# End of a recurrence in a hybrid decoder trunk: head norm in smaller parts, y turned and split in halves, two gate pieces last

## The chip, the core and the metric

The kernel runs on one core of a Trainium2 chip. The metric is the time of one execution on the device in microseconds (us), as the median of several runs. The engines are TensorE (PE, with PEld for its weight loads), VectorE (DVE), ScalarE (ACT), GpSimd (POOL) and SyncE (SP), which issues most DMAs. Line numbers (L112) are those of the kernel before.

## The reference

One layer of a decoder trunk on 1024 positions of width 1024, in float32. The input is normalized and projected once; the columns of the projection go to three branches and their gates. A branch is a recurrence over time (8 heads of 64), causal attention, or attention into 256 memory tokens. The branches are gated and merged, projected by w_out, and a convolutional feed-forward part follows.

```python
h = rms_norm(x, norm1_g[l])
proj = h @ w_in[l]
p_rwkv, p_sb, q_mem, gate_logits = jnp.split(proj, cut, axis=-1)
y_a, v_first = rwkv7_branch(p_rwkv, ...)
y_b = stick_breaking_branch(p_sb, ...)
y_m = memory_branch(q_mem, mem, ...)
ys = jnp.stack([y_a, y_b, y_m], axis=2)
branch_out = jnp.einsum('btnc,ncd->btnd', ys, w_branch[l])
gates = jax.nn.sigmoid(gate_logits.reshape(b, t, N_BRANCH, D_MODEL))
x = x + jnp.sum(gates * branch_out, axis=2) @ w_out[l]
x = x + conv_ffn(x, norm2_g[l], ...)
```

What matters here is the end of the first branch: the output y of the recurrence is normalized per head over 64 columns (mean and variance), scaled by lnx_g, shifted by lnx_b and a bonus term, and multiplied by a gate.

## The kernel before

A float32 matrix is split into a high and a low part, and each product takes three matmuls: high by high, high by low, low by high. PE runs nearly all of the time, and its order is written by hand: as long as `self.pin` is set, matmuls and transposes keep the order in which the program emits them. The order of the other engines is planned when the kernel is built: an instruction goes to its engine's list when the planner's clock says that its data and its buffer are there, earlier program text first.

The work before the merge is laid out as a main strand and a filler. The filler (`stream`, drawn through `pumped`) is a list of pieces of projections: a piece of 128 columns is eight steps of six matmuls of 512 columns (a gate piece, `gate_item`), or four such steps (a branch piece, `branch_item`). The main strand is a generator, and `weave` draws so many filler steps at each of its yields: 2.08 in the recurrence (`stage2`), 3 in `group_norm`. What is then left of the filler is drained. Each piece's weights are loaded one piece ahead by SP into one of two "wr" slots, and split by ACT (high part, L80) and POOL (low part, L81).

The recurrence (`stage2`) runs through 16 chunks of 64 positions, with three yields a chunk, for four tiles y[p] of two heads each (128 rows by 1024 columns: the rows are the positions of two chunks, and each group of 128 columns is one such pair of chunks for the two heads). After every fourth chunk `norm_quarter` normalizes the 256 columns that are then complete, in all four tiles: four reduces on DVE (L566), a scaling (L567), 16 squares with a running sum on ACT (L573), a power on POOL (L166, helper rsqrt), and 16 scalings of 64 columns on DVE (L580). It is a generator of ten steps, drawn one at a time at the yields of the next chunks. The last quarter follows chunk 15, drawn two steps at a yield, five yields in all.

`group_norm` turns a tile: eight transposes of 128 x 128 on PE (L105) into two PSUM banks, two multiplies by the loaded scale on DVE (L597), and one add of the loaded shift over 1024 columns (L598). Scale and shift come from DRAM by SP (L606, L607) into "at" buffers, of which there are seven. `branch_last` splits the turned tiles into a high part (ACT, L1094, in "at") and a low part (DVE, L1095, in "A", four buffers, which the low parts of branch 2 hold until its last matmul). Then it runs eight pieces of 128 columns with 24 matmuls each; DVE multiplies the result by the stored gate (L1183) and adds what the other branches gave (L1184), and ACT and DVE split it for w_out (L1190, L1191). `out_proj` follows, with its eight rows of w_out split into the slots that `load_wo` names. The text from `branch_last` to `out_proj` is not pinned.

A gate piece ends in a sigmoid. If its number (branch, piece) is in `stored`, ACT's queue stores it to DRAM (gsd, L738), and the branch piece that needs it loads it (L1117); if not, it stays in a "w4" buffer until its branch piece, which comes right behind it. The list `gq` gives the order in which the stored ones are made. A branch piece of branch 2 also loads the sum so far (mrd, L1120), multiplies (DVE, L1132), adds (POOL, L1134) and stores (POOL's queue, L1135). There are three "w4" buffers.

Of the kernel before, what the change touches and what calls it, by code (L numbers as in the profile page):

```python
# [49 lines left out]
class Trunk:  # L50
# [421 lines left out]
    def stage2(self):  # L472
        nc = self.nc
# [32 lines left out]
        for c in range(NC):  # L506
            g, cc = c // 2, c % 2
            us = []
            for p in range(4):
                L, (V, TT) = Ls[g, p], VTs[g, p]  # L510
                us.append((
                    U[p], L[:, cc * 128 : (cc + 1) * 128], L[:, 256 + cc * 128 : 256 + (cc + 1) * 128],
                    L[:, 512 + cc * 256 : 512 + (cc + 1) * 256], [v[:, cc * 64 : (cc + 1) * 64] for v in V],
                    TT[:, cc * 64 : (cc + 1) * 64], v1s[p], self.ps("g")))

            def state(o, rs):
                for p, h2 in heads if c else ():
# [12 lines left out]
            for p, h2 in heads:  # L530
                _, _, _, _, wv, tt, v1, pb = us[p]
                self.mmul(pb[hq[1 - h2], W], tt[hq[h2]], v1[hq[h2]], start=True, stop=True)
                if h2 == 1:
                    for q, w in zip(hq, wv[::-1]):
                        nc.scalar.activation(w[q], pb[q, W], AF.Copy)
            yield
            next(norm, None)
            state(Y, A)
            for p, (Up, ra, bt, M, wv, tt, v1, pb) in enumerate(us):
                for h2, q in enumerate(hq):  # L540
                    self.mmul(pb[q, Y], M[:, h2 * 128 : h2 * 128 + 64], wv[h2], start=(c == 0), stop=True)
                if c < NC - 1:
                    for h2, q in enumerate(hq):
                        self.mmul(pb[q, S], bt[:, q], wv[h2], start=True, stop=True)
                    nc.vector.scalar_tensor_tensor(Up, Up, self.pc[p][:, c : c + 1], pb[:, S], ALU.mult, ALU.add)
                for h2, q in enumerate(hq):
                    nc.scalar.activation(self.y[p][cc * 64 : cc * 64 + 64, g * 128 + h2 * 64 : g * 128 + h2 * 64 + 64], pb[q, Y], AF.Copy)
            if cc and g + 2 < NG:
                for p in range(4):
                    load(g + 2, p)  # L550
            yield
            next(norm, None)
            if c % 4 == 3:
                for _ in norm:
                    pass
                norm = self.norm_quarter(c // 4)
        for _ in norm:
            next(norm, None)
            yield

    def norm_quarter(self, i):
        nc = self.nc
        nm, vs = self.small("hn", [128, 16]), self.small("hn", [128, 16])
        ys = [y[:, i * 256 : (i + 1) * 256] for y in self.y]
        for p, y in enumerate(ys):
            nc.vector.tensor_reduce(nm[:, p * 4 : p * 4 + 4], y.rearrange("p (g i) -> p g i", i=64), AX.X, ALU.add)  # L566
        nc.vector.tensor_scalar(nm, nm, -1.0 / 64, None, ALU.mult)  # L567
        yield
        groups = [[(y[:, j * 64 : (j + 1) * 64], p * 4 + j) for j in range(4)] for p, y in enumerate(ys)]
        for gs in groups:  # L570
            for y, j in gs:
                junk = self.small("jk", [128, 64], bufs=1)
                nc.scalar.activation(junk, y, AF.Square, bias=nm[:, j : j + 1], accum_out=vs[:, j : j + 1])  # L573
            yield
        rs = self.small("hf", [128, 16], bufs=4)
        self.rsqrt(rs, vs, 16, 1.0 / 64, 64e-5)
        yield
        for gs in groups:
            for y, j in gs:
                nc.vector.tensor_scalar(y, y, nm[:, j : j + 1], rs[:, j : j + 1], ALU.add, ALU.mult)  # L580
            yield

    def group_norm(self):
        nc = self.nc
        self.yT, gs = [], []
        for p in range(3):
            gs.append(self.load_gg(p))
        yield
        for p in range(4):
            y = self.y[p]  # L590
            gg, bg = gs[p]
            for h in range(2):
                hs = slice(h * 512, (h + 1) * 512)
                pt = self.ps("g")
                for j in range(4):
                    self.transpose(pt[:, j * 128 : (j + 1) * 128], y[:, (h * 4 + j) * 128 : (h * 4 + j + 1) * 128])
                nc.vector.tensor_tensor(gg[:, hs], pt, gg[:, hs], ALU.mult)  # L597
            nc.vector.tensor_tensor(y, gg, bg, ALU.add)  # L598
            self.yT.append(y)
            if p == 0:  # L600
                gs.append(self.load_gg(3))
            yield

    def load_gg(self, p):
        gg, bg = self.t4("at"), self.t4("at")
        self.nc.sync.dma_start(gg, self.ggd[p, 0])  # L606
        self.nc.sync.dma_start(bg, self.ggd[p, 1])  # L607
        return gg, bg
# [472 lines left out]
                mid(s - 2)  # L1081
            yield

    def split_y(self, ys, last=False):
        nc = self.nc
        if last:
            his = [self.t4("at", F32R) for _ in ys]
        else:
            hi = self.pool_a.tile([128, 4, 1024], F32R, name=self.nm("yhi"), tag="inst")
            his = [hi[:, k] for k in range(4)]  # L1090
        out = []
        for hi, y in zip(his, ys):
            lo = self.t4("A", F32R)
            nc.scalar.activation(hi, y, AF.Copy)  # L1094
            nc.vector.tensor_tensor(lo, y, hi.bitcast(F32), ALU.subtract)  # L1095
            out.append((hi, lo))
        return out
# [51 lines left out]
        return load, items  # L1149

    def load_wo(self, k):
        slots = ["qk"] * 8 + ["at"] * 6 + ["it", "sp"]
        hl = [self.pool_l.tile([128, 1024], F32R, name="wo_sp", tag="sp", bufs=1) if s == "sp" else self.t4(s, F32R) for s in slots[2 * k : 2 * k + 2]]
        self.wo.append(self.split_raw(self.load_w(self.I["w_out"][k]), *hl))

    def branch_last(self):
        nc = self.nc
        self.wo = []
        y = self.split_y(self.yT, True)
        mg = lambda name, shape: self.pool_l.tile(shape, F32R, name=name, tag="l4")  # L1160
        self.mg0 = [[mg(f"mg0_{i}_{k}", [128, 2, 512]) for k in range(4)] for i in range(2)]
        self.mg1 = [[[mg(f"mg1_{i}_{t}_{k}", [128, 4, 256]) for k in range(2)] for t in range(2)] for i in range(2)]
        for d in range(8):
            if d % 2 == 0:
                w = self.split_w(self.I["w_br"][0, d // 2])
            g, o = self.t4("at"), self.t4()
# [1 line left out]
            nc.sync.dma_start(o, self.mrd[d])  # L1168
            pp = [self.ps("mm"), self.ps("mm")]
            if d == 0:  # L1170
                for i, (a, b) in enumerate(((0, 0), (1, 0), (0, 1))):
                    for k in range(4):
                        for h in range(2):
# [515 lines left out]
    def run(self):  # L1689
        nc, tc = self.nc, self.tc  # L1690
# [153 lines left out]
```

## Time and profile before

| what | us |
|---|---|
| median of 3 runs | 1870.23 |
| lowest, highest | 1868.52, 1876.17 |
| profiled execution | 1869.02 |
| its span, first to last instruction | 1867.2 |
| PE busy in the span | 1799.3 |
| mean granted TensorE clock | 0.988 |

A profile shows one execution. A timeline row gives start, length, engine, line, operation, output and inputs, the count of instructions merged into the row, and in brackets how long the engine was idle before and who released it. A row of the groups gives line, engine, operation, shapes and count, then the busy time and the mean length of one in ns, then the idle time of the engine just before. A row by stretch gives its length and the busy time of PE, PEld, DVE, ACT and POOL with the number of instructions, then the granted clock (1.00 is full), the DMA share and GB/s. A row of the DMA view gives target and source, queue, count, size of one, and the median time to landing.

### The profile page before, as it was taken

To read this page: it belongs to the slowest core of one execution; us is meant where nothing else is said; L and a number is where in the kernel's file an instruction comes from. 1 tells how busy PE (TensorE), PEld (TensorE's weight loads), DVE (VectorE), ACT (ScalarE), POOL (GpSimd) and SP (SyncE) were. 2 spreads that over 40 slices of the span, in tenths; PEclk is the share of its full clock that TensorE was granted. 3 is DMA by queue.
4 is the path that set the end of the run, shared out by engine and by line. 5 is a ranking of instruction groups with operands and counts; after the bars stand their busy time and mean duration, and the time that the engine had idled before them with its cause. 6 is when DMAs were issued, how large, how long until landed. Compare 5 with 4: busy or idle time off the path is not lost. (4 is left out here: it accounts for less than half of the span.)

```text
span 1867.2 us, 27381 instructions
## 1 busy us (share of the span) xinstructions
PE 1799.3 (96%) x10468; PEld 1451.9 (78%) x10468; DVE 1163.3 (62%) x1638; ACT 885.8 (47%) x1665; POOL 787.1 (42%) x448
## 2 busy tenths in 40 slices
PE   8999999999999999999999899979999999999999
PEld 6777778878787887787777688767888888878877
DVE  5656665998887423333333682467777677785586
ACT  5444343555565635534545433454444444554433
POOL 2323342322222452122233431487676767645454
PEclk9999999999999999999999999999999999999999
DMA  4155565111111432557744463222333233385475
GB/s 177 57 176 174 177 210 157 60 51 44 46 59 63 133 116 64 181 191 269 251 134 173 167 231 110 91 90 90 108 113 102 86 124 106 120 323 202 140 240 188
DMA packets 120037, 261.29 MB, mean 140 GB/s; under 512 B 28249, under 2 KB 40793, under 8 KB 119778
## 3 DMA queue, kind: packets, MB, share of 16 engines
q1 hardware_dynamic: 82434, 193.71, 31.7%
q10 hardware_dynamic: 33696, 53.23, 7.8%
q0 software_dynamic: 3776, 12.62, 2.1%
q8 instruction: 82, 1.34, 0.3%
q14 instruction: 49, 0.40, 0.1%
HBM read 178.99 MB, written 80.48 MB: 139 GB/s over the span
## 5 line engine op out<-in xcount | busy, mean ns | idle before, releaser
L81 POOL TENSOR_TENSOR wl<-wr,wh 128x1024 fp32r<-128x1024 f32 x77 | 195.2, 2536 | 499.3 <-ACT wh L80 499.2
L112 PE MATMUL mm<-xhi,wh 128*128 128x512 f32 x784 | 265.0, 419 | 9.6 <-ACT xhi L179 7.9
L112 PE MATMUL mm<-xlo,wh 128*128 128x512 f32 x784 | 246.6, 396 | 0.2 <-DVE xlo L180 0.2
L112 PE MATMUL mm<-xhi,wl 128*128 128x512 f32 x784 | 244.1, 393 | 0.4 <-POOL wl L81 0.3
L112 PEld LDWEIGHTS mm<-xlo,wh 128*128 128x128 f32 x784 | 149.3, 191 | 34.1 <-DVE xlo L180 0.9
L112 PEld LDWEIGHTS mm<-xhi,wl 128*128 128x128 f32 x784 | 148.5, 190 | 34.4 <-POOL wl L81 1.3
L112 PEld LDWEIGHTS mm<-xhi,wh 128*128 128x128 f32 x784 | 138.6, 192 | 40.5 <-issue 9.1
L80 ACT ACTIVATE wh<-wr 128x1024 fp32r<-128x1024 f32 x77 | 81.4, 1057 | 158.3 <-PE mm L112 84.5
L112 PE MATMUL mm<-dw,da 128*128 128x512 f32 x528 | 121.2, 390 | 1.5 <-DVE da L1584 1.4
L112 PE MATMUL mm<-BT,l 128*128 128x512 f32 x504 | 117.6, 389 | 0.0
L112 PE MATMUL mm<-BT,wh 128*128 128x512 f32 x352 | 110.0, 394 | 7.8 <-DVE u L1397 7.8
L112 PEld LDWEIGHTS mm<-dw,da 128*128 128x128 f32 x528 | 98.8, 188 | 23.3 <-DVE da L1584 2.3
L1585 POOL TENSOR_TENSOR dw<-draw,dw 128x512 fp32r<-128x512 f32 x55 | 81.1, 1482 | 84.8 <-ACT dw L1583 82.0
L831 DVE TENSOR_TENSOR_SCAN at<-at,at 128x128 f32<-128x128 f32 (+3 forms) x64 | 91.3, 1429 | 32.0 <-ACT at L825 31.9
L112 PE MATMUL mm<-B,wh 128*128 128x512 f32 x352 | 108.4, 389 | 2.1 <-ACT p L1439 2.1
L112 PEld LDWEIGHTS mm<-BT,l 128*128 128x128 f32 x504 | 94.6, 188 | 19.6
L1584 DVE TENSOR_TENSOR da<-draw,da 128x512 fp32r<-128x512 f32 x77 | 65.6, 860 | 61.2 <-ACT da L1582 60.6
L112 PE MATMUL g<-dw,da 128*128 128x512 f32 x396 | 92.2, 394 | 3.0 <-ACT dw L1583 1.9
L733 DVE TENSOR_TENSOR w<-w,rbc 128x1024 f32<-128x1024 f32 x24 | 49.2, 2049 | 68.7 <-ACT w L732 63.9
L1345 POOL TENSOR_TENSOR l<-it,l 128x1024 fp32r<-128x1024 f32 x21 | 50.8, 2419 | 95.3 <-ACT l L1344 95.3
L112 PEld LDWEIGHTS g<-dw,da 128*128 128x128 f32 x396 | 75.3, 190 | 19.4 <-ACT dw L1583 2.3
L1582 ACT ACTIVATE da<-draw 128x512 fp32r<-128x512 f32 x77 | 48.3, 628 | 83.8 <-PE mm L112 39.9
(326 smaller groups left out, 4002.2 us busy)
## 6 DMA issues: line engine op xcount, KB each, us to landing
wr<-in_w_in_dram SPq DMA_DIRECT2D x50, 512.0 KB, 3.6
draw<-actd SPq DMA_DIRECT2D x77, 256.0 KB, 3.6
at<-scr SPq DMA_DIRECT2D x28, 512.0 KB, 5.8
draw<-in_w_down_dram SPq DMA_DIRECT2D x55, 256.0 KB, 4.6
wr<-in_w_up_dram SPq DMA_DIRECT2D x22, 512.0 KB, 3.5
actd<-gall ACTq DMA_DIRECT2D x44, 256.0 KB, 3.0
rw<-in_w_up_dram SPq DMA_DIRECT2D x20, 512.0 KB, 3.7
gsd<-w ACTq DMA_DIRECT2D x18, 512.0 KB, 2.7
```

Source lines behind the costliest of these rows:

```text
L80: self.nc.scalar.activation(hi, raw, AF.Copy)
L81: self.nc.gpsimd.tensor_tensor(lo, raw, hi.bitcast(F32), ALU.subtract)
L112: self.pinned(self.nc.tensor.matmul(*a, **k))
L733: nc.vector.tensor_tensor(g, g, self.rbc, ALU.mult)
L831: self.pinned(nc.vector.tensor_tensor_scan(sn[:, :W][:, ::-1], sn[:, :W][:, ::-1], self.smask[:, 1024 - W :][:, ::-1], 1.0, ALU.mult, ALU. ...
L1345: nc.gpsimd.tensor_tensor(lo, src, hi.bitcast(F32), ALU.subtract)
L1582: self.pinned(nc.scalar.activation(A[:, 0], a, AF.Copy))
L1584: self.pinned(nc.vector.tensor_tensor(A[:, 1], a, A[:, 0].bitcast(F32), ALU.subtract))
L1585: nc.gpsimd.tensor_tensor(Wt[:, 1], w, Wt[:, 0].bitcast(F32), ALU.subtract)
```

## The change

The last quarter of the head norm becomes two parts. The norm now runs after chunks 3, 7, 11, 13 and 15, for column groups 0-1, 2-3, 4-5, 6 and 7, and what is left of a part when the next begins is issued at once. After chunk 13 the scale and shift of tiles 0 and 1 are loaded. The five yields behind chunk 15 go.

`group_norm` works in halves of 512 columns: first it turns half 0 of all four tiles (the add on POOL), then splits half 0 (high part in "qk", low part in "A"), then turns and splits half 1 tile by tile (the add on DVE). It has eleven yields, with one filler step at each. The fourth shift takes the "it" slot. `branch_last` takes these parts, and its first piece does columns 0 to 511 before 512 to 1023. `load_wo` uses the slots in another order. The gate pieces (2,2) and (2,3) are made among the stored ones, and (0,6) and (0,7) come last, behind branch 2.

```diff
-            if c % 4 == 3:
+            if c in (3, 7, 11, 13, 15):
                 for _ in norm:
                     pass
-                norm = self.norm_quarter(c // 4)
+                norm = self.norm_part(*{3: (0, 2), 7: (2, 4), 11: (4, 6), 13: (6, 7), 15: (7, 8)}[c])
+            if c == 13:
+                self.gs = [self.load_gg(p) for p in range(2)]
         for _ in norm:
-            next(norm, None)
-            yield
+            pass
...
     def group_norm(self):
         nc = self.nc
-        self.yT, gs = [], []
-        for p in range(3):
-            gs.append(self.load_gg(p))
+        gs = self.gs + [self.load_gg(2), self.load_gg(3, True)]
+        hl = [(self.t4("qk", F32R), self.t4("A", F32R)) for _ in range(4)]
+        self.yhl = hl
+
+        def turn(p, h, eng):
+            hs, (gg, bg), y = slice(h * 512, (h + 1) * 512), gs[p], self.y[p]
+            pt = self.ps("g")
+            for j in range(4):
+                self.transpose(pt[:, j * 128 : (j + 1) * 128], y[:, (h * 4 + j) * 128 : (h * 4 + j + 1) * 128])
+            nc.vector.tensor_tensor(gg[:, hs], pt, gg[:, hs], ALU.mult)
+            eng.tensor_tensor(y[:, hs], gg[:, hs], bg[:, hs], ALU.add)
+
+        def split(p, h):
+            hs, (hi, lo) = slice(h * 512, (h + 1) * 512), hl[p]
+            nc.scalar.activation(hi[:, hs], self.y[p][:, hs], AF.Copy)
+            nc.vector.tensor_tensor(lo[:, hs], self.y[p][:, hs], hi[:, hs].bitcast(F32), ALU.subtract)
+
         yield
         for p in range(4):
...
-            nc.vector.tensor_tensor(y, gg, bg, ALU.add)
-            self.yT.append(y)
-            if p == 0:
-                gs.append(self.load_gg(3))
-            yield
...
+            turn(p, 0, nc.gpsimd)
+            if p % 2:
+                yield
+        for p in range(4):
+            split(p, 0)
+            yield
+        for p in range(4):
+            turn(p, 1, nc.vector)
+            split(p, 1)
+            yield
...
-        slots = ["qk"] * 8 + ["at"] * 6 + ["it", "sp"]
+        slots = ["qk"] * 4 + ["at"] * 4 + ["qk"] * 4 + ["at"] * 2 + ["it", "sp"]
...
-        y = self.split_y(self.yT, True)
+        y = self.yhl
...
-                for i, (a, b) in enumerate(((0, 0), (1, 0), (0, 1))):
-                    for k in range(4):
-                        for h in range(2):
+                for h in range(2):
+                    for i, (a, b) in enumerate(((0, 0), (1, 0), (0, 1))):
+                        for k in range(4):
...
-        gq[14:14] = [(2, 0), (2, 1)]
+        gq[14:14] = [(2, d) for d in range(4)]
...
-        items += [lambda: drain(inv), ld1, gate(), gate(), gate(), mark("y1"), *br1, ld2, gate(), *br2]
+        items += [lambda: drain(inv), ld1, gate(), gate(), gate(), mark("y1"), *br1, ld2, gate(), *br2, gate(), gate()]
...
-        self.weave(self.group_norm(), pump, 3, 0)
+        self.weave(self.group_norm(), pump, 1.0, 0)
```

`norm_part(g0, g1)` is `norm_quarter` with 2 * (g1 - g0) heads' columns of 64 per tile in place of four, and reduce, scaling and power over as many.

More of the change, by code (lines that the diff above doesn't have):

```diff
@@ L575, in norm_quarter @@
         rs = self.small("hf", [128, 16], bufs=4)
-        self.rsqrt(rs, vs, 16, 1.0 / 64, 64e-5)
+        self.rsqrt(rs[:, : 4 * nh], vs[:, : 4 * nh], 4 * nh, 1.0 / 64, 64e-5)
         yield
@@ L584, in group_norm, with load_gg @@
         nc = self.nc
-        self.yT, gs = [], []
-        for p in range(3):
-            gs.append(self.load_gg(p))
+        gs = self.gs + [self.load_gg(2), self.load_gg(3, True)]
[12 more added lines that the diff above has]
+            nc.vector.tensor_tensor(lo[:, hs], self.y[p][:, hs], hi[:, hs].bitcast(F32), ALU.subtract)
         yield
         for p in range(4):
-            y = self.y[p]
-            gg, bg = gs[p]
-            for h in range(2):
[L593 to L598, printed above, removed]
-            self.yT.append(y)
-            if p == 0:
-                gs.append(self.load_gg(3))
-            yield
-    def load_gg(self, p):
-        gg, bg = self.t4("at"), self.t4("at")
+            turn(p, 0, nc.gpsimd)
[3 more added lines that the diff above has]
+            split(p, 0)
+            yield
+        for p in range(4):
+            turn(p, 1, nc.vector)
+            split(p, 1)
+            yield
+    def load_gg(self, p, last=False):
+        gg, bg = self.t4("at"), self.t4("it", n=1080)[:, :1024] if last else self.t4("at")
         self.nc.sync.dma_start(gg, self.ggd[p, 0])
@@ L1082, in mem_attn, with split_y @@
             yield
-    def split_y(self, ys, last=False):
+    def split_y(self, ys):
         nc = self.nc
[L1086 to L1090, printed above, removed]
+        hi = self.pool_a.tile([128, 4, 1024], F32R, name=self.nm("yhi"), tag="inst")
+        his = [hi[:, k] for k in range(4)]
         out = []
@@ L1170, in branch_last @@
             if d == 0:
-                for i, (a, b) in enumerate(((0, 0), (1, 0), (0, 1))):
-                    for k in range(4):
-                        for h in range(2):
+                for h in range(2):
+                    for i, (a, b) in enumerate(((0, 0), (1, 0), (0, 1))):
+                        for k in range(4):
                             self.mmul(pp[h], w[a][:, k * 256 : k * 256 + 128], y[k][b][:, h * 512 : (h + 1) * 512],
```

13 lines of the change are left out of this document (7 added, 6 removed).

## The prediction

> **What bounds the kernel now.** The page comes first: one core, and TensorE is the busy engine.
>
> ```profile
> span 1867.2 us, 27381 instructions
> PE 1799.3 (96%) x10468; PEld 1451.9 (78%) x10468; DVE 1163.3 (62%) x1638; ACT 885.8 (47%) x1665; POOL 787.1 (42%) x448
> ```
>
> PE is idle for 1867.2 - 1799.3 = 67.9 us in all, so a reordering can win only where PE waits or runs at a lower clock. The change touches the stretch from the end of the recurrence to the first branch; there the view of waits (waiter, releaser, total, times, longest) names who PE waits for.
>
> ```profile
> ACT at L1094 <- DVE qk L598: 7.4, 3, 2.6
> PE mm L112 <- ACT at L1094: 5.2, 3, 3.2
> ```
>
> Read backwards: PE waits for the high-part copy of y (ACT, L1094), which waits for the DVE add that finishes y (L598). The groups of PE from 1058.05 to 1080.42, and busy times by stretch (length, then PE, PEld, DVE, ACT, POOL, granted clock, DMA):
>
> ```profile
> L112 PE MATMUL mm<-at,wh 128*128 128x512 f32 x14 | 5.8, 539 | 5.2 <-ACT at L1094 5.2
> L112 PE MATMUL mm<-at,wl 128*128 128x512 f32 x12 | 4.9, 550 | 0.0
> L112 PE MATMUL mm<-A,wh 128*128 128x512 f32 x14 | 4.2, 428 | 1.0 <-DVE A L1095 1.0
> L105 PE MATMUL g<-kon,qk 128*128 128x128 f32 x16 | 2.3, 279 | 0.3 <-DVE at L597 0.3
> ```
>
> ```profile
> 1058.06:1080.43 22.37, 15.79 (x57) 11.08 (x56) 16.98 (x16) 6.89 (x7) 14.39 (x6) 0.77 0.69 233
> 1080.43:1114.88 34.45, 34.45 (x153) 28.53 (x152) 32.84 (x48) 13.09 (x26) 10.36 (x4) 1.00 0.67 229
> 1070.00:1075.00 5.00, 3.72 (x8) 2.52 (x9) 4.56 (x3) 1.30 (x2) 1.13 (x1) 0.50 0.93 298
> ```
>
> ```profile
> 1028.91 0.73 PE L112 MATMUL mm<-xhi,wh 128*128 128x512 f32 x2
> ...
> 1050.83 1.03 PE L105 MATMUL g<-kon,qk 128*128 128x128 f32 x8
> 1051.62 0.71 PE L112 MATMUL mm<-yhi,wh 128*128 128x512 f32 x2
> ...
> 1070.04 2.07 PE L112 MATMUL mm<-at,wh 128*128 128x512 f32 x4 [3.22 <-ACT at L1094]
> ```
>
> In the timeline of PE, 1028.91 is the first matmul behind the recurrence's last. What the stretch from 1058.06 costs: 40 matmuls (14 + 12 + 14) and 16 transposes took 22.37 us. At full clock a matmul of 512 columns takes 34.45 / 152 = 0.2266 us (one of the 153 is cut by the edge), and eight transposes 1051.62 - 1050.83 = 0.79 us. The same work needs 40 x 0.2266 + 2 x 0.79 = 10.65 us, so **11.7 us are lost**: 5.2 + 1.0 + 0.3 = 6.5 of waiting, and some 5.2 because the clock is at 0.50 after the 3.22 us gap. This is the ceiling for what a better end can give.
>
> [...]
>
> **The change, part by part.**
>
> *Where the cover goes.* One step of the pump is six matmuls, 6 x 0.2266 = 1.36 us. Groups of PE from 1028.90 to 1058.05 (three kinds of x24, three of x16; first and last):
>
> ```profile
> L112 PE MATMUL mm<-xhi,wh 128*128 128x512 f32 x24 | 7.5, 394 | 0.0
> L112 PE MATMUL mm<-A,wh 128*128 128x512 f32 x16 | 4.9, 390 | 0.0
> ```
>
> 72 + 48 = 120 matmuls: **20 steps** are left when the recurrence ends, and before, 16 of them stand ahead of the first transposes, so 4 are left for the rest. With the change 2 follow the last chunk, then one at each of group_norm's 11 yields, then 7. The PE order becomes: 3 steps, turn of half 0 of two tiles, 1, of the other two, 5, then four times (turn of half 1, 1 step), then 7. The turns of half 0 come at about 1028.9 + 3 x 1.36 = 1033; the first turn of half 1 after 9 steps and 16 transposes of 128 columns, at 1028.9 + 12.2 + 1.6 = **1042.7**; branch_last's first matmul at 1028.9 + 20 x 1.36 + 4 x 0.79 = **1059.3** (before: 1060.4). Since gates (0,6) and (0,7) close the stream, branch 2 ends with step 4 and frees the four A tiles that the low parts need, at about 1036. The number of matmuls, and of gate columns, is the same: (2,2) and (2,3) move ahead by what (0,6) and (0,7) fall back.
>
> *Is half 1 normalized in time?* Nothing in the trace is a last part of one column group; it is built from the last quarter's rows:
>
> ```profile
> 1029.15 1.83 DVE L566 TENSOR_REDUCE hn<-qk 128x4 f32<-128x256 f32 x4 [7.29 <-ACT qk L547]
> L573 ACT ACTIVATE jk<-qk,hn 128x64 f32<-128x64 f32 x16 | 5.6, 347 | 1.1 <-DVE hn L567 0.7
> L573 ACT ACTIVATION_READ_ACCUMULATOR jk<-qk,hn 128x1 f32 x16 | 3.0, 187 | 0.0
> L166 POOL TENSOR_TENSOR hf<-rs,half 128x16 f32<-128x16 f32 x1 | 2.9, 2927 | 1.8 <-DVE rs L165 1.8
> L166 POOL TENSOR_TENSOR hf<-rs,half 128x8 f32<-128x8 f32 x5 | 8.3, 1668 | 30.3 <-DVE rs L165 30.2
> 1044.92 5.74 DVE L580 TENSOR_SCALAR qk<-qk,hn,hf 128x64 f32<-128x64 f32 x16 [2.45 <-POOL hf L166]
> ```
>
> Before: reduces from 1029.15, scaling until 1044.92 + 5.74 = 1050.7, so 21.5 us. New: four reduces 0.9 to 1.8 (half the columns), eight squares 8 x (0.347 + 0.187) = 4.3, the power 1.7 (eight columns), and of the scalings only the first two for the first turn, 2 x 5.74 / 16 = 0.7; two more DVE steps on a few columns cost less than a reduce (0.46 each). That is 7.6 to 9.4, from 1029.15 to 1037 or 1039. Other work of these engines in between, two ACT copies or one POOL split (rows below: 2.1, 2.6), makes 1041. Against 1042.7: **no wait**; bounds 0 to 2.6 us. The extra part in chunks 14 and 15 adds four reduces and eleven short steps beside the recurrence; most of it stands in place of work that came later, and I take 0.3 us (0 to 2).
>
> *Turn and split.* Uncontended rows, and the nearest one for the add that moves to POOL:
>
> ```profile
> L597 DVE TENSOR_TENSOR at<-g,at 128x512 f32<-128x512 f32 x4 | 2.6, 684 | 0.8 <-PE g L105 0.8
> L598 DVE TENSOR_TENSOR qk<-at,at 128x1024 f32<-128x1024 f32 x2 | 2.4, 1216 | 0.0
> L1585 POOL TENSOR_TENSOR dw<-draw,dw 128x512 fp32r<-128x512 f32 x55 | 81.1, 1482 | 84.8 <-ACT dw L1583 82.0
> L598 DVE TENSOR_TENSOR qk<-at,at 128x1024 f32<-128x1024 f32 x4 | 7.9, 2003 | 0.0
> ```
>
> Half 1 of a tile costs DVE the multiply, 0.68, the add and the low part's subtraction (an instruction of the same form), half of 1.22 each: 1.9 us, 7.6 for four, from 1042.7 on, and the last turn is at 1048.0: ready at about 1051, while the seven steps last until 1059.3. The first piece of branch_last now takes columns 0 to 511 first (12 matmuls, 2.7 us), so half 1 may come as late as 1062. Half 0's splits lie wholly under the steps before. The cover is 8 us; if it is gone, each us beyond it is a us of PE. The reason for late data would be DVE against POOL: the last row is the add of the second one over all four tiles, at a mean of 2003 ns; in the stall POOL is busy 14.39 of 22.37 us. POOL gains four adds, 4 x 1.48 = 5.9 us. I take 0.7 us of PE loss (0 to 6).
>
> [...]
>
> *Loads.* load_gg of tiles 0 and 1 moves up into chunk 13, two loads each on SP, where it stands ahead of the next mrd and w_br loads and waits for the at buffers of chunks 12 and 13 to come free, so SP cannot issue it much earlier than before; those behind it have a piece, 8 us (below), to land. The fourth bias takes the "it" slot and no longer waits for a free "at". Two more gate stores (ACT's queue) and two more gate loads (SP), 512 KB each, are wanted a piece or more later. I take 0 for all; a load that is late by its whole landing costs what the starved pieces do.
>
> *w_out slots.* Rows 4 and 5 of w_out now sit in the slots of the high parts of y, free only when branch_last's last matmul is done:
>
> ```profile
> 1114.88 11.36 PE L112 MATMUL mm<-qk,mg 128*128 128x512 f32 x48
> 1126.08 8.32 PE L112 MATMUL mm<-at,mg 128*128 128x512 f32 x36
> 1115.90 5.20 POOL L81 TENSOR_TENSOR at<-wr,at 128x1024 fp32r<-128x1024 f32 x2 [2.34 <-ACT at L80]
> wr<-in_w_out_dram SPq DMA_DIRECT2D x8, 512.0 KB, 3.8
> L80 ACT ACTIVATE wh<-wr 128x1024 fp32r<-128x1024 f32 x77 | 81.4, 1057 | 158.3 <-PE mm L112 84.5
> ```
>
> The first w_out matmul is at 1114.88. Row 4 is wanted 48 matmuls after that, 11.2 us. An ACT copy of 1.1 and POOL at 2.6 each make rows 4 and 5 ready after 3.7 and 6.3; row 6 follows a load of 3.8 and another 3.7, at 11.2, wanted at 16.4. Cost 0 (to 8 if POOL or the queue slips), cover 5 us.
>
> Sum: -11.7 + 0.3 + 0.7 = **-10.7 us**. The profiled execution took 1869.0 us (span 1867.2); this gives 1858.3 there, and from the median 1870.2 it gives **1859.5**.
>
> **The rivals.**
>
> *Starved pieces of branch 2 (slower).* Pieces (2,0) to (2,3) now follow each other with stored gates; before only two did. Each needs two w4 buffers of three.
>
> ```profile
> 902.06 0.73 PE L112 MATMUL mm<-yhi,wh 128*128 128x512 f32 x2
> 910.26 0.73 PE L112 MATMUL mm<-yhi,wh 128*128 128x512 f32 x2
> 909.82 2.39 POOL L1134 TENSOR_TENSOR w<-w,w 128x1024 f32<-128x1024 f32 x1 [5.60 <-DVE w L1132]
> 920.48 2.37 POOL L1134 TENSOR_TENSOR w<-w,w 128x1024 f32<-128x1024 f32 x1
> mrd<-w POOLq DMA_DIRECT2D x16, 512.0 KB, 5.2
> w<-mrd SPq DMA_DIRECT2D x16, 512.0 KB, 6.0
> ```
>
> PE needs 910.26 - 902.06 = 8.2 us a piece. If multiply (two halves at L597's 0.68), add 2.4, store 5.2 and load 6.0 of one piece must pass before the next, that is 15.0, a slip of 6.8 for three successions, 20.4; PSUM's four banks hide one piece, 8.2. PE then idles 12.2, and at the ratio of the stall above (11.7 lost for 6.5 waited) loses 22: 1869.0 - 10.7 + 22 = 1880, in the median 1881. Against it: the two that stood together were 10.66 us apart on POOL, a slip of 2.5, 7.4 for three, less than 8.2. It decides from 2.7 us of slip a piece.
>
> [...]
>
> *The wait only moves.* PE stands still at the first piece as before, since DVE and POOL have the same work to do in fewer us: 1870. For it: DVE is 4.56 of 5.00 busy in the stall. Against it: seven steps of cover.
>
> *w_out late.* PE waits up to 8 us at row 4 or 6: 1867.5.
>
> **How the numbers follow.** About 0.5% (9.4 us, below 1860.9) can be told from no change. Forecast 0.62, its own range 1857 to 1862.5, of which 0.55 is beyond 0.5%; half 1 late 0.14 (0.01 of it beyond 0.5%); only moved 0.07; w_out late 0.05; starved pieces 0.12 (0.02 within 0.5%). So faster 0.55 + 0.01 = 0.56, slower 0.10, within 0.5% 0.07 + 0.13 + 0.07 + 0.05 + 0.02 = 0.34. The range 1856.5 to 1869.0 leaves out the starved pieces, part of "only moved" and the lower edge of the forecast, about 0.18.
>
> **What would show it.** Right: no PE wait for the copies of y, the granted clock at 1.00 from the recurrence's end to w_out, the first-branch matmuls begin some 30 us after the last recurrence matmul and run 43.5 us without a gap. The norm step: the last scaling ends before 1045. [...] Wrong: PE waiting at (2,2) to (2,4) for a multiply; a wait of a turn for the last scaling; a PE gap at row 4 of w_out; or a total near 1870 with the wait at a new line.

## The result, and the profile after

| | median us | lowest, highest | ratio to before (95% interval) |
|---|---|---|---|
| before | 1873.15 (19 runs beside the changed kernel) | 1866.8, 1877.1 | 1 |
| changed | 1879.68 (19 runs) | 1871.9, 1884.0 | 1.0036 (1.0025 to 1.0048) |

The changed kernel is **slower by 0.36%**, 6.5 us between the medians; 10.7 us of gain were forecast. Line numbers of the changed kernel are shifted: L566 is now L568 (reduces), L573 L575 (squares), L580 L582 (scalings), L597 and L598 L596 and L597 (multiply and add of a turn), L1094 and L1095 L601 and L602 (high and low parts of y), L1132, L1134, L1135 are L1142, L1144, L1145 (multiply, add and store of a piece of branch 2), L1183, L1184, L1191 are L1193, L1194, L1201 (multiply, add and low part in branch_last).

The page of the changed kernel (profiled execution 1880.29 us), and busy times over branch_last, from its first matmul to the first one of w_out (length; then PE, PEld, DVE, ACT, POOL; granted clock, DMA share, GB/s):

```profile
span 1878.2 us, 27413 instructions
PE 1803.9 (96%) x10468; PEld 1456.1 (78%) x10468; DVE 1172.9 (62%) x1648; ACT 887.8 (47%) x1669; POOL 786.8 (42%) x453
```

```profile
1073.09:1117.06 43.97, 43.94 (x194) 35.96 (x192) 37.93 (x48) 19.03 (x32) 18.44 (x8) 1.00 0.71 243
```

The aimed-at stall is gone: branch_last runs 43.97 us at full clock without a gap, and no wait for a copy of y is left. PE's idle time is 1878.2 - 1803.9 = 74.3 us, though, against 67.9 before. The timeline of PE in the changed kernel shows where the new waits stand; 1035.70 is the first matmul behind the recurrence.

```profile
887.61 0.81 PE L112 MATMUL g<-ys,at 64*64 64x64 f32 x8 [2.93 <-ACT qk L547]
...
950.59 1.12 PE L112 MATMUL g<-ys,qk 64*64 64x64 f32 x16 [3.54 <-DVE ys L527]
...
1004.65 0.72 PE L112 MATMUL g<-ys,qk 64*64 64x64 f32 x16 [1.53 <-DVE ys L527]
...
1035.70 0.73 PE L112 MATMUL mm<-yhi,wh 128*128 128x512 f32 x2
...
1056.39 0.47 PE L105 MATMUL g<-kon,qk 128*128 128x128 f32 x1 [4.66 <-DVE qk L582]
...
1121.43 5.88 PE L112 MATMUL mm<-qk,mg 128*128 128x512 f32 x18 [2.85 <-DVE at L1193]
...
1188.72 1.40 PE L105 MATMUL g<-kon,w 128*128 128x128 f32 x8 [2.08 <-ACT w L1238]
```

The same places before:

```profile
884.84 0.95 PE L112 MATMUL g<-ys,at 64*64 64x64 f32 x8 [2.90 <-ACT qk L547]
...
940.38 1.75 PE L112 MATMUL g<-ys,at 64*64 64x64 f32 x16 [1.23 <-ACT qk L547]
...
999.59 0.72 PE L112 MATMUL g<-ys,qk 64*64 64x64 f32 x16 [0.96 <-DVE ys L527]
...
1182.23 1.09 PE L105 MATMUL g<-kon,w 128*128 128x128 f32 x8 [2.08 <-ACT w L1228]
```

By the copies of L527, four to a chunk, the first three waits of the changed kernel stand in chunks 5, 9 and 13, counted from 0 as the program does. The recorded expectations below call these places chunks 7, 8 and 12.

With these rows the 11.0 us between the two spans can be laid out. A wait starts at its row's time less the number in brackets.

| stretch | before | changed | difference |
|---|---|---|---|
| start to the wait in chunk 5 | 881.94 | 884.68 | +2.7 |
| from there to the end of the recurrence | 147.0 | 151.0 | +4.0 |
| to the first w_out matmul (1114.88, 1117.06) | 86.0 | 81.4 | -4.6 |
| to the wait at the transposes of w | 65.3 | 69.6 | +4.3 |
| to the end of the span | 687.0 | 691.6 | +4.5 |

In the first line and in the last PE has the same work in both kernels. The last took 685 to 692 us in the executions below, whatever the edit, so these two lines are spread between executions; a single span can't decide a few us here, and the verdicts below go by the ratios. **The three lines between are the change**, 3.7 us together: a wait of 3.54 in chunk 9 where before 1.23 stood, one of 1.53 in chunk 13 for 0.96, a part of the gain lost again at the turn of half 1 (4.66), and a new wait of 2.85 at w_out. The medians differ by 6.5 us; where the other 3 us arise these rows don't show.

Who is behind them? POOL's timeline in the changed kernel, and then before:

```profile
941.62 2.38 POOL L1144 TENSOR_TENSOR w<-w,w 128x1024 f32<-128x1024 f32 x1 [0.45 <-DMA w<-mrd]
944.30 0.57 POOL L1145 DMA_DIRECT2D mrd<-w  x1 [0.30 <-POOL w L1144]
944.89 2.93 POOL L166 TENSOR_TENSOR hf<-rs,half 128x16 f32<-128x16 f32 x1
...
1046.05 2.40 POOL L1144 TENSOR_TENSOR w<-w,w 128x1024 f32<-128x1024 f32 x1
1048.40 1.29 POOL L597 TENSOR_TENSOR qk<-at,at 128x512 f32<-128x512 f32 x1
1049.63 0.57 POOL L1145 DMA_DIRECT2D mrd<-w  x1
1050.23 2.51 POOL L597 TENSOR_TENSOR qk<-at,at 128x512 f32<-128x512 f32 x2
1052.70 2.13 POOL L166 TENSOR_TENSOR hf<-rs,half 128x8 f32<-128x8 f32 x1
...
1114.63 5.53 POOL L81 TENSOR_TENSOR qk<-wr,qk 128x1024 fp32r<-128x1024 f32 x2 [11.44 <-PE mm L112]
```

```profile
939.83 2.92 POOL L166 TENSOR_TENSOR hf<-rs,half 128x16 f32<-128x16 f32 x1 [2.02 <-DVE rs L165]
948.09 2.39 POOL L1134 TENSOR_TENSOR w<-w,w 128x1024 f32<-128x1024 f32 x1 [5.33 <-DVE w L1132]
```

And DVE in the changed kernel:

```profile
937.59 1.29 DVE L1142 TENSOR_TENSOR w<-mm,w 128x512 f32<-128x512 f32 x2 [5.42 <-DMA w<-gsd]
...
942.26 1.77 DVE L165 TENSOR_SCALAR rs<-hn 128x16 f32<-128x16 f32 x1 [1.81 <-ACT jk L575]
947.86 2.54 DVE L582 TENSOR_SCALAR qk<-qk,hn,hf 128x64 f32<-128x64 f32 x11 [3.83 <-POOL hf L166]
950.32 0.60 DVE L527 COPY ys<-g 128x64 f32<-128x64 f32 x4
...
1038.72 0.85 DVE L568 TENSOR_REDUCE hn<-qk 128x2 f32<-128x128 f32 x4
...
1044.46 1.65 DVE L165 TENSOR_SCALAR rs<-hn 128x8 f32<-128x8 f32 x1 [0.64 <-ACT jk L575]
...
1054.86 2.81 DVE L582 TENSOR_SCALAR qk<-qk,hn,hf 128x64 f32<-128x64 f32 x8 [1.56 <-POOL hf L166]
...
1115.23 5.55 DVE L1201 TENSOR_TENSOR mg<-at,mg 128x512 fp32r<-128x512 f32 x3
1120.70 1.27 DVE L1193 TENSOR_TENSOR at<-mm,at 128x512 f32<-128x512 f32 x2
```

DVE before, and what SP's loads of the stored gates (L1127) wait for in the changed kernel, from 895 to 955:

```profile
939.59 0.17 DVE L165 TENSOR_SCALAR rs<-hn 128x16 f32<-128x16 f32 x1
```

```profile
SPq L1127 <- DMA mrd<-w: 13.0, 2, 6.5
```

Two theories come from these rows. **The first: the norm's power stands behind other work in POOL's list.** Before, the power (L166) of the norm part behind chunk 7 ran at 939.83 and the add of branch 2 at 948.09. Now the add and its store stand first, the power follows at 944.89, the scalings on DVE wait for it (3.83 us), and the copy that the recurrence needs (L527) stands behind the scalings on DVE: PE waits 3.54 us. The add also holds up the step ahead of the power: L165 on DVE takes 1.77 us beside it and 0.17 before. And it is late itself. SP issues the loads of the stored gates only when stores of the sum are through (13.0 us of waiting), and the add ahead of this one, at 933.95, had waited 6.38 us for its load of the sum. At the turn of half 1, an add of branch 2, three adds of half 0 and a store stand between 1046.05 and the power at 1052.70. **The second: at w_out, POOL splits rows 4 and 5 one right behind the other** (5.53 us from 1114.63), the three low parts on DVE take 5.55 us beside them, the multiply behind these starts only at 1120.70, and it is what frees the PSUM banks that w_out's matmuls wait for. Rivals: the norm in parts and the early loads cost the recurrence its 4 us; and DVE is late at w_out through its own work.

### The profile page after: what moved, and what is told of

It reads as the page before. It is cut to its first block, busy times and chain, and to the rows that moved or that the text cites. A ratio compares the mean times of both kernels' runs of the same rounds, so it can differ in the third digit from the quotient of the medians.

```text
span 1878.2 us, 27413 instructions
## 1 busy us (share of the span) xinstructions
PE 1803.9 (96%) x10468; PEld 1456.1 (78%) x10468; DVE 1172.9 (62%) x1648; ACT 887.8 (47%) x1669; POOL 786.8 (42%) x453
## 5 line engine op out<-in xcount | busy, mean ns | idle before, releaser
L80 ACT ACTIVATE wh<-wr 128x1024 fp32r<-128x1024 f32 x77 | 81.4, 1057 | 147.7 <-PE mm L112 85.8
L112 PEld LDWEIGHTS mm<-BT,wh 128*128 128x128 f32 x352 | 67.3, 192 | 22.7 <-DVE u L1407 8.7
```

The costliest lines, as they stand in the source:

```text
L80: self.nc.scalar.activation(hi, raw, AF.Copy)
L112: self.pinned(self.nc.tensor.matmul(*a, **k))
```

## Experiments

Ratios are to the kernel before, run beside each on the same chip. The changed kernel's, 1.0036, is the base.

**The list undone, all else kept** (h1), and **the list alone in the kernel before** (h2).

```diff
-gq[14:14] = [(2, d) for d in range(4)]
+gq[14:14] = [(2, 0), (2, 1)]
-items += [..., *br1, ld2, gate(), *br2, gate(), gate()]
+items += [..., *br1, ld2, gate(), *br2]
```

> The changed kernel with the list of pieces of before: only (2,0) and (2,1) stored ahead, no gates after branch 2. Norm in parts, turn in halves and the new slots stay. Theory (the order of the pieces is what costs in the recurrence): the waits for ys in chunks 8 and 12 go, the recurrence from its first matmul to its last takes 206 us and not 210; but the low parts of y must wait for the last piece of branch 2, so a wait of 2 to 6 us can come back at the end. Rival (the norm in parts and the earlier loads cost it): the recurrence stays at 210 us.

> The kernel before with nothing changed but the list of pieces: (2,0) to (2,3) stored ahead, the gates (0,6) and (0,7) after branch 2. Theory (the list alone makes POOL's adds of the merged sum and their stores stand ahead of the norm's power): PE waits for ys at chunk 8 (3 to 5 us) and chunk 12 (about 1.5 us) appear, c. 147 us from the wait of chunk 7 to the last recurrence matmul become 151 to 154, and the kernel is 2 to 5 us slower than before at its end (1875 to 1878), unless the early A tiles shorten the stall of 6.5 us behind the recurrence. Rival (the earlier loads of gg or the norm in parts are needed for it): the recurrence stays at 147.

Measured: h1 1871.22 us, ratio 0.9992 (0.9978 to 1.0007); h2 1882.60 us, 1.0045 (1.0028 to 1.0062). The timeline of PE in h1:

```profile
945.06 1.76 PE L112 MATMUL g<-ys,at 64*64 64x64 f32 x16 [1.23 <-ACT qk L547]
...
1004.38 0.72 PE L112 MATMUL g<-ys,qk 64*64 64x64 f32 x16 [0.96 <-DVE ys L527]
...
1091.79 1.01 PE L112 MATMUL mm<-qk,wh 128*128 128x512 f32 x2 [2.31 <-DVE at L1193]
...
1118.42 1.82 PE L112 MATMUL mm<-qk,mg 128*128 128x512 f32 x3 [2.86 <-DVE at L1193]
```

and POOL's in h1:

```profile
944.51 2.93 POOL L166 TENSOR_TENSOR hf<-rs,half 128x16 f32<-128x16 f32 x1 [2.02 <-DVE rs L165]
952.77 2.41 POOL L1144 TENSOR_TENSOR w<-w,w 128x1024 f32<-128x1024 f32 x1 [5.33 <-DVE w L1142]
```

PE in h2:

```profile
951.70 1.12 PE L112 MATMUL g<-ys,qk 64*64 64x64 f32 x16 [4.97 <-DVE ys L527]
```

In h1 the power stands ahead of the add again, and the waits of chunks 9 and 13 are those of before; the wait for the turn of half 1 has gone too. From the wait of chunk 5 to the recurrence's end it takes 147.7 us. In h2 the list alone brings the waits, 4.97 in chunk 9 and 1.53 in chunk 13, this stretch takes 152.6 us, and it loses more than I expected since a first matmul of branch_last waits there too (2.57 us for ACT's copy of a gate piece out of PSUM, L732, since two gates now come last). It costs 0.44% in the changed kernel (1.0036 to 0.9992) and 0.45% in the one before: **8 us either way** in the medians (3.5 and 7.3 us in the traces, from the wait in chunk 5 to the transposes of w), so it is the list and neither the norm in parts nor the early loads. h1 pays a part back in branch_last, though hardly through late low parts of y, as I expected (0.45 us): PE waits 2.31 us for the multiply of the third piece (L1193), which frees the PSUM banks. On DVE the low parts of the second piece (L1201) stand ahead of it. They wait 2.27 us for ACT's copies, which stand behind the split of a row of w_out whose load is late (2.59 us), and then take 4.38 us beside two splits on POOL.

**Two other ways to the same wait.** The four stored pieces spread out (e3), and branch 2's adds on DVE (f3):

```diff
-gq[14:14] = [(2, d) for d in range(4)]
+gq[14:14] = [(2, 0), (2, 1), (2, 4), (2, 6)]            # e3
-            nc.gpsimd.tensor_tensor(g, g, o, ALU.add)
+            (nc.vector if b == 2 else nc.gpsimd).tensor_tensor(g, g, o, ALU.add)   # f3
```

> The changed kernel, but the four pieces of branch 2 whose gates are stored ahead are (2,0), (2,1), (2,4), (2,6) and not (2,0) to (2,3), so that at most two stand next to each other. Theory (pieces in a row pull the add of the merged sum and its store on POOL ahead of the norm's power, and PE waits for ys behind it in chunks 8 and 12): the two waits of the recurrence for ys, 3.54 and 1.53 us, go, and the kernel is about 4 to 5 us faster (1875). Rival (the waits come from the norm's own length, whatever stands beside it): both waits stay within 1 us and the time stays at 1879.

> The changed kernel, but branch 2's adds of the merged sum run on DVE and not on POOL; the stores stay on POOL. Theory (the power stands behind the add, 2.4 to 2.7 us, more than behind the store): the wait for ys at chunk 8 falls from 3.5 to 5.2 us to 2 or less, that at chunk 12 is gone, that of the turn of half 1 falls from 4.66 to about 2.2, and the kernel is some 5 us faster than the changed one (1874). Rival (POOL waits for data, so that it's the store and its source that hold the power): the waits stay at 3 us or more.

Measured: e3 1875.56 us, 1.0015 (1.0000 to 1.0030); f3 1873.94 us, 1.0000 (0.9990 to 1.0010). In e3 both waits for ys are gone (1.23 and 1.36 us for ACT's copies stand there), while the turn still waits 4.66 and w_out 2.51. In f3 the waits are smaller, not gone (chunk 13: 1.19). From the wait in chunk 5 to the recurrence's end e3 takes 150.2 us and f3 150.1, though, against 151.0 in the changed kernel and 147.0 before: neither gives the recurrence its time back. PE and then DVE in f3:

```profile
944.39 1.43 PE L112 MATMUL g<-ys,at 64*64 64x64 f32 x12 [2.23 <-ACT qk L547]
...
1054.14 0.33 PE L105 MATMUL g<-kon,qk 128*128 128x128 f32 x1 [2.83 <-DVE qk L582]
```

```profile
942.44 1.22 DVE L1144 TENSOR_TENSOR w<-w,w 128x1024 f32<-128x1024 f32 x1 [5.20 <-DMA w<-mrd]
```

The add, now on DVE, waits 5.20 us for its load of the merged sum: pieces with stored gates in a row leave the loads too little time, as the 5.42 us for w<-gsd in the changed kernel say already. By these rows the list works in two steps: the loads make the adds late, and the late add stands in front of other work, of the power on POOL and, in f3, of a step of the recurrence itself on DVE (L545 at 943.58). Whether the new order would cost anything with its loads in time wasn't tried.

**Half 0's adds on DVE** (e4), `turn(p, 0, nc.gpsimd)` made `turn(p, 0, nc.vector)`.

> The changed kernel, but half 0's four adds of the turn run on DVE and not on POOL. Theory (in POOL's queue two of these adds, 2.4 and 2.5 us, stand ahead of the power of the last part's norm): the wait of the first turn of half 1 for the scaling, 4.66 us, shrinks to 1.5 us or less, and the kernel is 3 to 5 us faster (1875 to 1877). Rival (the wait is set by the add of branch 2 and its store, or by DVE, which now has 2.7 us more to do): it stays above 3.5 us and the time within 1 us.

Measured: 1877.32 us, 1.0020 (1.0006 to 1.0033). The turn's wait falls from 4.66 to 1.54 us, as expected; the interval overlaps that of the changed kernel, so that a gain of 2.4 us in the medians isn't clear of noise. What is left has two sources: on POOL branch 2's add and store end at 1052.45, and on DVE two of the moved adds take 5.70 us beside POOL's work, so that the step before the power (L165) starts only at 1052.06. PE:

```profile
1055.97 0.33 PE L105 MATMUL g<-kon,qk 128*128 128x128 f32 x1 [1.54 <-DVE qk L582]
```

**Low parts of rows 4 and 5 of w_out on DVE** (e2).

```diff
-        self.wo.append(self.split_raw(self.load_w(self.I["w_out"][k]), *hl))
+        self.wo.append(self.split_raw(self.load_w(self.I["w_out"][k]), *hl, nc.vector if k in (4, 5) else None))
```

> The changed kernel, but the low parts of rows 4 and 5 of w_out are subtracted on DVE and not on POOL. Theory (POOL splits these rows just as branch_last ends, and DVE's last copies stand still beside it, 5.55 us for three): the wait of 2.85 us of the w_out matmuls for the copy of the merged piece (L1193) falls below 0.5 us and their 18 matmuls go back from 5.88 to about 4.1 us, so that the kernel is some 4.5 us faster than the changed one (about 1875). Rival (DVE is late there by its own work, and two more subtractions of 1.2 us on it make that worse): the wait stays at 2.5 us or more and the time does not fall.

Measured: 1871.83 us, 0.9995 (0.9977 to 1.0012). DVE, then PE in e2:

```profile
1120.07 1.36 DVE L1201 TENSOR_TENSOR mg<-at,mg 128x512 fp32r<-128x512 f32 x3
```

```profile
1121.39 5.60 PE L112 MATMUL mm<-qk,mg 128*128 128x512 f32 x24
```

DVE has 2.4 us more to do and is through earlier: the same three low parts take 1.36 us and not 5.55, and PE runs into w_out without a wait. From the first w_out matmul to the transposes of the next stage it is 27.2 us, as before (27.5), against 31.9 in the changed kernel: 4.6 us, as expected. The medians differ by more, 0.41% or 7.7 us; the 3 us beyond are within the spread of such a comparison, and I have no other cause for them.

**Both repairs** (k5: old list, rows 4 and 5 on DVE), and **all eight rows on DVE** (k4).

> The changed kernel with the old list of pieces and with the low parts of rows 4 and 5 of w_out on DVE. Theory (the two costs, of the list and of the rows, are independent and add): from 1871.2 (old list alone) the wait of 2.86 us at the w_out matmuls goes with its half clock: 1866 to 1868, below before. Rival (with one wait gone another engine is late at the next place): 1870 or more, with a new wait behind 1115.

> The changed kernel with the old list of pieces and the low parts of all eight rows of w_out on DVE. Theory (DVE's multiplies are late in branch_last only because DVE stands still beside pairs of POOL splits: three low parts took 4.38 us beside two splits and 1.36 alone): both waits for L1193, 2.31 and 2.86 us, go, and it runs in 1863 to 1866, faster than with rows 4 and 5 alone. Rival (DVE has too much of its own work in branch_last, and 8 subtractions of 1.2 us more make it the bound): the wait at the third piece of branch_last grows above 3 us and the time is above that with rows 4 and 5 alone.

Measured: k5 1867.08 us, **0.9963 (0.9947 to 0.9980)**; k4 1869.88 us, 0.9976 (0.9964 to 0.9987). k5 is below both kernels. From the single effects, 1.0036 - 0.0044 - 0.0041 = 0.9951 would follow; the two add up to within the interval. One wait is left in branch_last, 2.39 us for the multiply of its third piece. In k4 it grew. PE, then DVE in k4:

```profile
1089.35 1.01 PE L112 MATMUL mm<-qk,wh 128*128 128x512 f32 x2 [3.43 <-DVE at L1193]
```

```profile
1087.38 1.23 DVE L81 TENSOR_TENSOR at<-wr,at 128x1024 fp32r<-128x1024 f32 x1 [3.41 <-ACT at L80]
```

My theory lost here, and not quite to the rival that I wrote: DVE isn't too busy, it is blocked. A row's subtraction waits for ACT's copy, which waits for the row's load, and the multiply that PE needs (at 1088.52) stands behind it. The medians of k4 and k5 can't be told apart; it is the traces that show the longer wait.

**The same, with a row's split issued behind its piece's multiplies** (k6): `load_wo(d - 2)` moved below the loop over the halves.

> As the kernel with the old list and all rows of w_out on DVE, but the split of a row is issued behind the multiplies and low parts of its piece and not ahead of them. Theory (with all rows on DVE, the third piece was late because a row's subtraction stood at the head of DVE's queue for 3.41 us, waiting for its load): the wait for L1193 in branch_last, 3.43 us, falls below 1 us, and it runs in 1863 to 1866. Rival (DVE's own work in branch_last is too long, or the sub of a row that is late now delays the next piece): the wait is 2 us or more, time 1868 or more.

Measured: 1869.51 us, 0.9981 (0.9968 to 0.9994); the wait is 3.90 us. The theory fell: one place later, the late row still stands ahead of the next piece's multiply (3.69 us of waiting for ACT's copy). Here a row whose load isn't in does less harm on POOL (2.39 us in k5), which PE isn't waiting for.

**The last quarter of the norm undivided** (k9: k5 with one part of two column groups behind chunk 15).

> As the kernel with the old list and rows 4 and 5 on DVE (1867.1), but the last quarter of the norm is not divided: one part of two column groups behind chunk 15, as before. It tests the step of the prediction that divides the norm. If the smaller last part is what gets half 1 there in time: 32 scalings of 0.36 us and a power of 2.9 us stand behind the recurrence again, the turns wait 4 to 8 us for the scaling, and the kernel takes 1871 to 1876. Rival (POOL's queue alone decides, and with the old list there is room): no wait of a turn above 1 us, and the time within 2 us of 1867.1, or below it because chunk 14 and 15 are free of the extra part (the recurrence 1 us shorter).

Measured: 1876.06 us, 1.0025 (1.0011 to 1.0039), 0.62% or 11.6 us above k5. PE:

```profile
1051.84 0.92 PE L105 MATMUL g<-kon,qk 128*128 128x128 f32 x2 [6.80 <-DVE qk L582]
```

The turn waits 6.80 us, and a low part of y another 2.26 (1078.36). From the wait of chunk 5 to the recurrence's end k9 takes 147.2 us and before 147.0; the four kernels with the old list and the extra part (h1, k5, k4, k6) take 147.7 to 149.2. So the extra part costs 0.5 to 2.2 us there, and is well worth it.

**The changed kernel's own list with three repairs** (k1: adds of branch 2, adds of half 0 and rows 4 and 5, all on DVE), and **another list** (k10: (2,0), (2,1), (2,6), (2,7) stored; adds of (2,6) and (2,7), of half 0, and rows 4 and 5 on DVE).

> The changed kernel with its own new list, but branch 2's adds, half 0's adds of the turn and the low parts of rows 4 and 5 all on DVE, so that nothing but stores and weight splits stands in POOL's queue ahead of the powers. Theory (POOL's queue and its pairs beside DVE are the whole loss, and the three repairs add): from the changed kernel's 1879.7 the three single repairs gave 5.7, 2.4 and 7.8 us: 1864 to 1868, the turn's wait at most 0.5 us, no wait at w_out. Rival (they overlap, or DVE becomes late instead): 1870 or more, with waits for DVE's multiplies L1142 or L1193.

> The changed kernel with the pieces stored ahead (2,0), (2,1), (2,6) and (2,7): the recurrence sees the same order of pieces as before up to (2,5), and the gates (0,6) and (0,7) still close the stream. The adds of (2,6) and (2,7), half 0's adds of the turn, and the low parts of rows 4 and 5 run on DVE. Theory (all the loss of the change comes from the order at POOL and its splits beside DVE): 147 to 148 us from the wait of chunk 7 to the last recurrence matmul and no wait for ys above 1.3 us, the turn of half 1 waits 1 us or less, no wait above 1 us in branch_last and none at w_out; the kernel is at 1861 to 1866, below the kernel before and below the two best so far (1867.1 and 1868.7). Rival (the two stored pieces side by side behind the recurrence are starved, or DVE is late with the multiplies there): a wait for L1142 or a turn of 2 us or more, 1868 or above.

Measured: k1 1868.68 us, 0.9976 (0.9964 to 0.9988); k10 1868.96 us, 0.9970 (0.9956 to 0.9984). k1 confirms the two costs that come after the recurrence: the turn waits 0.65 us, PE at most 0.47 for a multiply in branch_last, and w_out not at all. The recurrence it doesn't mend: that stretch takes 151.7 us (151.0 in the changed kernel), with 2.40 us of waiting at chunk 9, where DVE's add waits 5.40 us for its load. Its time lies between theory and rival (1864 to 1868, or 1870). k10 keeps the recurrence at 148.2 us, but the turn still waits 4.58 us. PE, then DVE in k10:

```profile
1053.43 0.33 PE L105 MATMUL g<-kon,qk 128*128 128x128 f32 x1 [4.58 <-DVE qk L582]
```

```profile
1046.38 1.23 DVE L1144 TENSOR_TENSOR w<-w,w 128x1024 f32<-128x1024 f32 x1 [3.18 <-DMA w<-mrd]
```

Here the rival was right: two stored pieces side by side behind the recurrence wait for the merged sum, and on DVE the step before the power (L165) stands behind that. The intervals of k5, k1 and k10 overlap; which of them is best isn't settled.

## Why the prediction was wrong

- **The ceiling, 11.7 us of stall: right.** It went; branch_last runs as forecast, 43.97 us against "43.5 us without a gap", though it begins 37.4 us after the recurrence and not "some 30". Without its list and with rows 4 and 5 on DVE (k5) the change gains 0.37%, 6.9 us, of the 10.7 forecast; the 2.39 us of waiting for the third piece's multiply, and half clock behind it (37 matmuls and not 46 in the ten us from 1090, at a mean granted clock of 0.83), are of the size of the 3.8 us that are missing.
- **"(2,2) and (2,3) move ahead", loads "I take 0 for all": this step failed, and it costs most**, 8.2 us in the medians (h1, h2). I counted matmuls and asked whether a piece's loads come in time for PE, not what else a late load holds up. Before, the power ran at 939.83 and the add at 948.09; the moved pieces bring an add, late by its loads, in front of the power. Putting the add on DVE takes the block along (150.1 us in f3 and 151.7 in k1, from the wait in chunk 5 to the recurrence's end); the lists that leave the order up to (2,5) as it was get the time back (147.7 in h1, 148.0 in k5, 148.2 in k10).
- **"No wait" for half 1, bounds 0 to 2.6: failed.** From the first reduce to the scaling it should be 7.6 to 9.4 us, some 12 with other work; it was 16.1, from 1038.72 to 1054.86. The squares and the power's own length (2.13 for 1.7) were about as reckoned; L165 took 1.65 us beside a split on POOL. The first reduce also came 3.0 us after the recurrence's end and not 0.2, behind a gate piece's multiply on DVE (2.42 us). The term that failed is "other work of these engines in between, one POOL split": 6.6 us of adds and stores stood there, from 1046.05 to 1052.70. Three adds of half 0 among them, 1.29 + 2.51 us, are the change's own; I had priced them only for what they take from DVE, 1.48 each. k9 shows that the idea of the step, dividing the norm, is right: with the old list and rows 4 and 5 on DVE it is worth 11.6 us.
- **"Cost 0 (to 8 if POOL or the queue slips), cover 5 us" for the w_out slots: failed**, 4.6 us in the trace (2.85 of waiting, the rest at half clock: 18 matmuls take 5.88 us and not 4.1), 7.7 in the medians (e2). Rows 4 and 5 were in time for their matmuls, as I worked out. What I left out is what their split does to DVE: work on POOL beside DVE, which I weighed for the adds of half 0, comes here as two POOL splits just when the last merged pieces need DVE (three low parts in 5.55 us, and in 1.36 in e2). The bound of 8 held, the reason given for it didn't.
- **The extra part at 0.3 us (0 to 2)**: 0.5 to 2.2 us in the recurrence (h1, k5, k4 and k6 against k9 and before), more than the 0.3 and up to its upper bound.
- **The rivals.** "Starved pieces" had the sign and nearly the total (1881 against 1879.7), and its loads are in fact late (5.42 us for w<-gsd). But PE never waits at (2,2) to (2,4) for a multiply, nor do PSUM's banks run out; the loads delay an add, and the add a power. That the totals agree is luck. The rival charged 22 us on one chain and so forecast 11 us more than before; measured are 6.5, and the totals meet because the median of before was 1870.2 then and 1873.15 beside the changed kernel. Forecast and result are 17.2 us apart, and this comes from several places: the list and the rows together 13.7 (1.0036 to 0.9963 in k5), and 3.8 of gain not reached. "Half 1 late", which I gave 0.14, happened as well, mainly through POOL's list and not through the norm's length or through DVE being slower beside POOL, and so did a late w_out, at its PSUM banks and not at row 4. I gave each a chance on its own, as if one excluded the others; three happened together.

## What to carry to other kernels

When pieces of work are moved, write down each engine's list around the instruction with the shortest way to the critical engine, here a power of 2.9 us on GpSimd, and ask what now stands ahead of it and whether its loads will be in; busy shares (POOL 42%) don't show it. A buffer slot that comes free at the end of a stage also fixes when the work that fills it runs, and so whom it collides with: two GpSimd splits at the wrong moment cost 4.6 us at w_out, as much as the change had won on the way there. Moving a blocked instruction to another engine moves the block along with it, unless what it waits for (here a load, 5.20 us in f3) comes earlier.

## What the runs showed of the hardware

Three low parts on DVE take 1.36 us in e2, and in the changed kernel 5.55 us beside two POOL splits of 5.53 us together (2.76 from 1114.63, 2.80 from 1117.36). The first two of them one by one:

```profile
1115.23 2.71 DVE L1201 TENSOR_TENSOR mg<-at,mg 128x512 fp32r<-128x512 f32 x1
1117.87 2.57 DVE L1201 TENSOR_TENSOR mg<-at,mg 128x256 fp32r<-128x256 f32 x1
```

Each of the two ends shortly behind the split that began ahead of it, 0.55 us in the first case (1117.94 against 1117.39) and 0.28 in the second (1120.44 against 1120.16), so here two splits in a row delayed DVE twice; the third, with no split ahead, takes 0.41 us.

The clock also fell after short waits. Two stretches and, below each, the one that follows it: first in the kernel before, around the wait of 1.23 us at 940.38, then in the changed kernel, around that of 1.53 us at 1004.65:

```profile
938.60:942.01 3.41, 1.76 (x21) 0.93 (x21) 1.15 (x6) 2.69 (x9) 2.18 (x1) 1.00 0.49 154
942.01:945.42 3.41, 3.41 (x26) 2.81 (x23) 2.63 (x12) 0.00 (x0) 0.75 (x1) 0.50 0.02 5
```

```profile
1001.63:1005.05 3.42, 1.89 (x19) 1.31 (x18) 3.42 (x18) 0.02 (x1) 0.00 (x0) 1.00 0.39 144
1005.05:1008.46 3.41, 3.41 (x30) 2.58 (x26) 0.16 (x1) 2.24 (x9) 0.00 (x0) 1.00 0.00 0
```

The shorter wait was followed by half clock and the longer one was not. The stretches are cut where the trace lets the clock change: in the trace of the kernel before and in that of the changed one, all changes lie on a fixed grid of 3.41 us, and half clock lasts 3.41, 6.83 or 10.24 us (the last time in each trace is cut off by its end). What comes next goes with how busy PE was over the whole stretch and not with one wait. Over these two traces, from the first record of the clock on (13.58 and 15.18 us), at full clock and with PE busy for less than 43% of a stretch, half clock followed in all 16 cases, from 43 to 54% in 3 of 8, above that in 2 of 1034; busy time alone doesn't decide it. A wait of 2.08 us at the same transposes was followed by a slow row in the changed kernel (1.40 us for eight, at half clock from 1189.36) and not before (1.09). PE idle for half of such a stretch was enough at 938.60 (1.76 us busy of 3.41), so a wait can cost more than its own length: behind the 2.85 us at w_out the granted clock is 0.50 from 1121.10 to 1124.51. Over the 19 executions of the changed kernel the longer ones tend to have the lower clock: the fastest, 1871.89 us, has a mean granted clock of 0.989, the slowest, 1884.00 us, 0.983.
